# Paced early weight splits, four chunk buffers, spread bias broadcasts and a turned mask product in a two-model forward pass

## The chip, the cores and the metric

One core of one Trainium2 chip runs the kernel. The metric is the device time of one execution in microseconds (us), less being better; a run before the change and a run after it are measured in the same way. The core has a matrix engine (TensorE, PE in the profile; its weight loads are shown apart as PEld), a vector engine (VectorE, DVE), an activation engine (ScalarE, ACT), a general engine (GpSimd, POOL) and a synchronisation engine (SyncE, SP). SP issues most of the DMAs here, POOL and ACT a few.

## The reference, cut to what matters

Two models run one after the other on one sequence of 512 tokens of width 1024, in float32.

```python
def first_block(x, ...):                       # layer 0: short convolution, layer 1: NSA attention
    for layer in range(2):
        h = rms_norm(x, norm_mix[layer])
        x = x + (short_conv_mixer(h, ...) if layer < 1 else nsa_mixer(h, ...))
        x = x + squared_relu_mlp(rms_norm(x, norm_mlp[layer]), mlp_w1[layer], mlp_w2[layer])
...
def ssd_chunked(x, dt, a, bmat, cmat):         # 5 chunks of 128 positions, 4 groups of 8 heads of 64
    cs = jnp.cumsum(dtc * a.reshape(SSD_GROUPS, SSD_HPG), axis=2)
    lmat = jnp.exp(jnp.where(causal, cs_t[..., :, None] - cs_t[..., None, :], -jnp.inf))
    cb = jnp.einsum('bclgn,bcsgn->bcgls', cc, bc)
    y_diag = jnp.einsum('bcgls,bcgrls,bcsgrp->bclgrp', cb, lmat, xdt)
    ...
    return (y_diag + y_off).reshape(bsz, lp, SSD_HEADS, SSD_HEADDIM)

def second_block(x, ...):                      # 16 meta tokens in front, then one layer
    h = h + valid_h * mixer_block(h, ...)      # SSD and sliding-window attention, gated and merged
    h = h + valid_h * conv_ffn(h, ...)
```

The bias of the attentions depends on the distance of two positions alone (`t5_bucket`), so a row of biases by distance per head is enough; every row of a tile takes it shifted by one.

## The kernel before, in words

**Products.** Activations lie with their 1024 features over eight tiles of 128 partitions and the 512 tokens along the free axis. A product keeps float32 accuracy by three products of rounded parts: every operand is split into a high part and a rest, and `mm3` (L305 is where it issues them) does high by high, rest by high and high by rest. `gemm` makes one 128-feature output tile from the k tiles of a weight in two halves of four (half a chunk each). A matmul reads its weights (the stationary operand) first: in the trace `mm<-hh,whi` has the moving operand's tile and then the weight's.

**The weight stream.** All big weights lie in one tensor of 362 chunks of 128x1024 float32 (512 KB), in the order of use. `Stream.pre` (from L178) is called ahead of each half: SP loads the chunk into `w32` (name `w` in the trace, two buffers, up to two chunks ahead, L188), ACT rounds a half into `whi` (L207, L200), and DVE makes `wlo = w - whi` (L209); whi and wlo have four buffers and run up to three halves ahead of the half in use.

**The early split.** `Stream.ahead` (L147 to L175) is called once for a chunk of the stream, from the tenth chunk on, in layer A and in both MLPs. At three calls of four it takes one later chunk out of `todo` (those of the NSA attention, 96 to 132, and of the second model's mixer, 197 to 271: 112 in all): POOL loads it into `aw` (L161), ACT rounds it to `ah` (L172; L168 where a scale is folded in, in pieces), DVE makes `al` (L173, L169), and POOL stores `al` to a DRAM tensor `dlo` (L174). When the chunk's turn comes, SP loads `wlo` from `dlo` (L197) and DVE is spared. Tiles `aw` and `al` have two buffers, `ah` one.

**The order.** The program is written in loops, and a scheduler that plays a timeline orders each engine's instructions; what is pinned (`keep_in_program_order`) stays in the order written. The engines run their own lists strictly in that order.

**The stages.** By the trace: layer A (short convolution, `layer_a`) to 224 us, MLP 0 to 587, NSA attention to 940, MLP 1 to 1315, preparation and window attention of the second model to 1510, its SSD cores (with the attention's output and further projections laid between as filler) to some 1910, merge to 2090, feed-forward layer to 2474.

**The bias broadcasts.** In layer A `biases` (from L600) makes one row of biases per head (`line`, in DRAM), and POOL then copies each of the 16 rows to 128 rows of DRAM three times (`sk1`, `sk2`, `sk3`; 320, 192 and 72 KB; L622, named `sk<-line` in the trace), with a pitch one longer than the row, so that later reads come out shifted.

**The SSD core.** Per group of eight heads, `core` first adds the part of earlier chunks into `y4` (positions on partitions, L1527). Per head it then makes the decay mask: PE spreads the head's cumulated sums over 128 partitions (`s<-csT,indr`, a 64x512 product, L305), ACT takes the difference and its exponent (L1542, L1544: tile `L`, two buffers), POOL multiplies by the shared matrix (L1545), `split` makes `Mh` and `Ml` (one buffer each). For each of four chunks, PE takes Mh and Ml as weights of 128 columns (`u<-xd,Mh`, 128 columns moved; `u<-xd,Ml`, 64). DVE adds the two halves of `u` into `y4` (L1555, L1556). After every second head PE turns `y4` (`o<-ckt,y`), and DVE adds it to `xs` with the skip term (L1562). PSUM holds two `u` tiles.

Of the kernel before, what the change touches and what calls it, by code (L numbers as in the profile page):

```python
# [19 lines left out]
P = 128  # L20
# [28 lines left out]
AHEAD0 = 10  # L49
# [76 lines left out]
class Stream:  # L126
# [13 lines left out]

    def scaled(self, half):
        g, ks = self.plan[half]
        n = 512 // len(ks)
        for i, k in enumerate(ks):
            yield slice(i * n, i * n + n), self.b.pv(g, k)

    def ahead(self):  # L147
        if self.ap is None or not self.todo or self.nd < AHEAD0:
            return
        self.owed += 3  # L150
        if self.owed < 4:
            return
        self.owed -= 4
        nc = self.b.nc
# [7 lines left out]
        if 2 * c in self.plan or 2 * c + 1 in self.plan:  # L162
            for o in range(2):
                e = slice(o * 512, o * 512 + 512)
                ws, hs, ls = w[:, e], h[:, e], l[:, e]
                parts = self.scaled(2 * c + o) if 2 * c + o in self.plan else [(slice(0, 512), 1.0)]
                for a, sc in parts:
                    nc.scalar.activation(out=hs[:, a], in_=ws[:, a], func=AF.Copy, scale=sc)  # L168
                    nc.vector.scalar_tensor_tensor(out=ls[:, a], in0=ws[:, a], scalar=sc, in1=hs[:, a].bitcast(F32),  # L169
                                                   op0=ALU.mult, op1=ALU.subtract)  # L170
        else:
            nc.scalar.activation(out=h, in_=w, func=AF.Copy)  # L172
            nc.vector.tensor_tensor(out=l, in0=w, in1=h.bitcast(F32), op=ALU.subtract)  # L173
# [10 lines left out]
    def pre(self, half):  # L184
        b, nc = self.b, self.b.nc
        while self.nd < min(self.nch, half // 2 + 2):
            t = self.pool.tile([P, 1024], F32, tag="w32", name="w32", bufs=2)
            nc.sync.dma_start(t, self.src[self.nd])  # L188
            self.w32[self.nd] = t
            self.nd += 1  # L190
# [41 lines left out]
class Builder:  # L232
# [230 lines left out]
    def first(self):  # L463
# [15 lines left out]
        with ExitStack() as c:  # L479
# [3 lines left out]
            self.st.ap = c.enter_context(tc.tile_pool(name="ahead", bufs=1))  # L483
# [3 lines left out]
            if self.stop == "a":  # L487
                return
            self.mlp("mlp_w1_0", "mlp_w2_0", "g_mlp0")
# [17 lines left out]
    def layer_a(self):  # L507
# [14 lines left out]
        for f in range(KD):  # L522
            pcs = []
            for part in (1, 2, 0):
                if f == 0 and part:
                    p = (p1, p2)[part - 1]
                else:
                    p = self.ps1()
                    self.gemm([(p, XS)], "a_w_in", 0, part * 1024 + f * 128, hs)
                pcs.append(p)  # L530
# [26 lines left out]
        for m in range(KD):  # L557
            p = self.ps1()
            self.gemm([(p, slice(0, 512))], "a_w_out", 0, m * 128, ys)
            x = self.xs[m]  # L560
# [39 lines left out]
    def biases(self):  # L600
# [19 lines left out]
        for h in range(16):  # L620
            for sk, a, n in ((self.sk1, 0, 640), (self.sk2, OH_A, 384), (self.sk3, OH_A + 384, 144)):
                nc.gpsimd.dma_start(sk[h:h + 1, :].rearrange("o (q w) -> (o q) w", w=n + 1)[:, 0:n],  # L622
                                    self.line[h:h + 1, a:a + n].to_broadcast([128, n]))
# [719 lines left out]
    def dt_unit(self, tp):  # L1343
# [60 lines left out]
        self.csT = ap.tile([64, W], F32R, name="csT")  # L1404
        pt = self.mmb()
        for c in range(4):
            self.tr(pt[0:32, c * 128:c * 128 + 128], cs[:, c * 32:c * 32 + 32])
        nc.scalar.activation(out=self.csT[0:32, 16:528], in_=pt[0:32], func=AF.Copy)
        nc.vector.tensor_tensor(out=self.csT[32:64, 16:528], in0=pt[0:32], in1=self.csT[0:32, 16:528].bitcast(F32),
                                op=ALU.subtract)  # L1410
# [18 lines left out]
    def ssd(self, c):  # L1429
# [13 lines left out]
        def core(g):  # L1443
# [77 lines left out]
            for cx in range(4):  # L1521
# [8 lines left out]
                if cx < 3:  # L1530
# [4 lines left out]
                    nc.vector.tensor_tensor(out=prev, in0=prev, in1=po, op=ALU.add)  # L1535
            for i in range(8):
                h = 8 * g + i
                s = self.sb()
                self.mm(s, self.indr[0:64, h:h + 1].to_broadcast([64, P]), self.csT[:, XS], True, True)
                L = t5("L", 2, "L")  # L1540
                for cx in range(4):
                    nc.scalar.activation(out=L[:, cx * 128:cx * 128 + 128], in_=s[:, cx * 128:cx * 128 + 128], func=AF.Relu,  # L1542
# [4 lines left out]
                self.split(Mh, Ml, L)  # L1547
                u = self.ub()
                for cx in range(4):
                    cc = slice(cx * 128, cx * 128 + 128)  # L1550
                    self.mm(u[:, cc], Mh[:, cc], xds[cx][:, i].rearrange("p a b -> p (a b)"), True, False)
                    self.mm(u[:, cx * 128:cx * 128 + 64], Ml[:, cc], xds[cx][:, i, 0, :], False, True)
                uv = u.rearrange("p (c b) -> p c b", b=128)
                yv = y4[:, :, i * 64:i * 64 + 64]
                nc.vector.tensor_tensor(out=yv, in0=uv[:, :, 0:64], in1=yv, op=ALU.add)  # L1555
                nc.vector.tensor_tensor(out=yv, in0=uv[:, :, 64:128], in1=yv, op=ALU.add)  # L1556
                if i % 2:
                    t = i // 2
                    po = self.ob()
                    for cx in range(4):  # L1560
                        self.tr(po[:, cx * 128:cx * 128 + 128], y4[:, cx, t * 128:t * 128 + 128])
                    nc.vector.scalar_tensor_tensor(out=xs[t][:, XS], in0=xs[t][:, XS], scalar=self.pv("dsk", 4 * g + t),  # L1562
                                                   in1=po, op0=ALU.mult, op1=ALU.add)
# [317 lines left out]
```

## Time and profile before, and how to read it

| | us |
|---|---|
| median of three runs | 2486.36 |
| the three runs | 2483.63, 2486.36, 2491.55 |
| the profiled execution, its own time | 2476.05 |
| its span, first to last instruction | 2474.3 |
| PE busy | 2391.7 |
| DVE busy | 1624.5 |
| ACT busy | 1231.0 |
| POOL busy | 471.5 |

A profile has one execution. Its tables give busy time per engine, the work in stretches of the span, what an engine waited for, and the start of each instruction. In a stretch of uniform products, the number of matmuls by the spacing of an undisturbed stretch is the time PE needs; what the stretch took beyond that was lost. Idle time of an engine that is not the bottleneck costs nothing by itself.

### The profile page before, as it was taken

What the parts mean: (1) busy time and instruction counts of PE and PEld (TensorE: products, weight loads), DVE (VectorE), ACT (ScalarE), POOL (GpSimd) and SP (SyncE); (2) the same over time, 40 slices, a digit from 0 to 9 for tenths busy, and PEclk for the clock granted to TensorE, in tenths of its full rate; (3) what the DMA queues carried; (4) which work ended last, traced back from release to release, by engine and by line L of the source; (5) the groups of instructions that cost most, each with busy time, mean ns of one, the idle gap of its engine ahead of it and who ended that gap; (6) DMA issues with size and microseconds to landing.
All of it is one profiled execution on the core that took longest, in us unless ns stands there. A gap on an engine that the chain in (4) does not pass through costs nothing.

```text
span 2474.3 us, 38734 instructions
## 1 busy us (share of the span) xinstructions
PE 2391.7 (97%) x14273; PEld 2078.8 (84%) x14273; DVE 1624.5 (66%) x3293; ACT 1231.0 (50%) x2431; POOL 471.5 (19%) x657
## 2 busy tenths in 40 slices
PE   7999999999899999999999999999999999999997
PEld 5777777887787777777888999999999999998996
DVE  8657855543777768746636895569776566864873
ACT  6436543333677765434344776556555334432442
POOL 2333221001333322221022222122322100000001
PEclk9999999999999999999999999999999999999998
DMA  7898886335743347887335354543335452333322
GB/s 277 271 266 289 303 306 223 95 117 166 242 129 93 120 144 255 297 283 278 103 94 195 114 149 148 166 152 121 125 125 162 141 196 86 95 94 94 92 88 77
DMA packets 151739, 418.93 MB, mean 169 GB/s; under 512 B 22603, under 2 KB 29003, under 8 KB 151499
## 3 DMA queue, kind: packets, MB, share of 16 engines
q1 hardware_dynamic: 115024, 287.70, 36.3%
q0 software_dynamic: 35392, 127.49, 15.4%
q8 instruction: 112, 1.84, 0.3%
q10 hardware_dynamic: 1132, 1.26, 0.2%
q14 instruction: 79, 0.65, 0.1%
HBM read 340.62 MB, written 83.23 MB: 171 GB/s over the span
## 4 chain that ended last, share of the span: by engine, by line
PE 67%; issue 17%; POOL 5%; DMA 4%; DVE 4%; ACT 2%; POOLq 0%; DVEq 0%; SPq 0%; ACTq 0%
PE mm L305 53%; PE g L305 4%; PE o L305 3%; PE s L305 2%; DMA sk<-line 2%; POOL aw L161 2%; POOL dlo L174 2%; PE u L305 1%; DMA aw<-in_ws_dram 1%; PE pt L309 1%; PE u L309 1%; DVE e L728 1%; DMA w<-in_ws_dram 1%; ACT ph L313 0%; POOL acc L339 0%
## 5 line engine op out<-in xcount | busy, mean ns | idle before, releaser
L305 PE MATMUL mm<-hh,whi 128*128 128x258 f32 (+2 forms) x2464 | 799.0, 325 | 23.2 <-ACT hh L353 11.6
L305 PE MATMUL mm<-hh,wlo 128*128 128x258 f32 (+2 forms) x2464 | 798.7, 324 | 4.5 <-DVE wlo L209 4.5
L305 PE MATMUL mm<-hl,whi 128*128 128x258 f32 (+2 forms) x2464 | 798.8, 324 | 4.3 <-DVE hl L354 4.3
L207 ACT ACTIVATE whi<-w 128x512 fp32r<-128x512 f32 x500 | 308.5, 626 | 499.1 <-PE mm L305 322.7
L305 PEld LDWEIGHTS mm<-hh,whi 128*128 128x128 f32 x2464 | 464.5, 189 | 70.5 <-ACT hh L353 15.4
L209 DVE TENSOR_TENSOR wlo<-w,whi 128x512 fp32r<-128x512 f32 x498 | 347.9, 702 | 242.7 <-ACT whi L207 235.3
L305 PEld LDWEIGHTS mm<-hh,wlo 128*128 128x128 f32 x2464 | 465.3, 189 | 48.8 <-DVE wlo L209 7.4
L305 PEld LDWEIGHTS mm<-hl,whi 128*128 128x128 f32 x2464 | 465.1, 189 | 46.8 <-DVE hl L354 6.1
L305 PE MATMUL mm<-a,whi 128*128 128x512 f32 (+1 forms) x699 | 275.5, 395 | 5.1 <-ACT whi L207 4.7
L305 PE MATMUL mm<-a,wlo 128*128 128x512 f32 (+1 forms) x699 | 276.2, 395 | 3.8 <-DVE wlo L209 3.5
L305 PE MATMUL mm<-b,whi 128*128 128x512 f32 (+1 forms) x699 | 275.3, 394 | 1.8 <-DVE b L314 1.8
L173 DVE TENSOR_TENSOR al<-aw,ah 128x1024 fp32r<-128x1024 f32 x91 | 111.4, 1224 | 125.8 <-ACT ah L172 125.6
L172 ACT ACTIVATE ah<-aw 128x1024 fp32r<-128x1024 f32 x91 | 96.3, 1059 | 176.9 <-DMA aw<-in_ws_dram 169.2
L305 PEld LDWEIGHTS mm<-a,wlo 128*128 128x128 f32 x699 | 132.6, 190 | 38.5 <-DVE wlo L209 8.8
L305 PEld LDWEIGHTS mm<-a,whi 128*128 128x128 f32 x699 | 132.5, 189 | 37.4 <-ACT whi L207 6.9
L200 ACT ACTIVATE whi<-w 128x512 fp32r<-128x512 f32 x182 | 114.0, 630 | 97.1 <-PE mm L305 88.4
L305 PEld LDWEIGHTS mm<-b,whi 128*128 128x128 f32 x699 | 132.6, 190 | 32.2 <-DVE b L314 2.4
L174 POOL DMA_DIRECT2D dlo<-al x112 | 60.5, 540 | 440.1 <-DVE al L173 324.0
L305 PE MATMUL mm<-oh,whi 128*128 128x258 f32 (+1 forms) x400 | 123.8, 311 | 2.3 <-ACT oh L313 2.1
L305 PE MATMUL mm<-ol,whi 128*128 128x258 f32 (+1 forms) x400 | 124.2, 310 | 0.3 <-DVE ol L314 0.3
L305 PE MATMUL mm<-oh,wlo 128*128 128x258 f32 (+1 forms) x400 | 123.4, 308 | 0.0
L305 PEld LDWEIGHTS mm<-oh,whi 128*128 128x128 f32 x400 | 76.8, 193 | 7.7 <-ACT oh L313 2.4
(541 smaller groups left out, 4292.3 us busy)
## 6 DMA issues: line engine op xcount, KB each, us to landing
w<-in_ws_dram SPq DMA_DIRECT2D x361, 512.0 KB, 4.1
aw<-in_ws_dram POOLq DMA_DIRECT2D x112, 512.0 KB, 6.3
dlo<-al POOLq DMA_DIRECT2D x112, 512.0 KB, 4.3
wlo<-dlo SPq DMA_DIRECT2D x224, 256.0 KB, 2.9
sk<-line POOLq DMA_DIRECT2D x16, 320.0 KB, 9.4
bias<-sk SPq DMA_DIRECT2D x16, 256.0 KB, 3.2
sk<-line POOLq DMA_DIRECT2D x16, 192.0 KB, 9.7
x<-xs SPq DMA_DIRECT2D x8, 264.0 KB, 2.8
```

The lines of the kernel that those rows point to most:

```text
L161: nc.gpsimd.dma_start(w, self.src[c])
L172: nc.scalar.activation(out=h, in_=w, func=AF.Copy)
L173: nc.vector.tensor_tensor(out=l, in0=w, in1=h.bitcast(F32), op=ALU.subtract)
L174: nc.gpsimd.dma_start(self.dlo[c], l.bitcast(F32))
L200: nc.scalar.activation(out=h[:, a], in_=src[:, a], func=AF.Copy, scale=sc)
L207: nc.scalar.activation(out=h, in_=src, func=AF.Copy)
L209: eng.tensor_tensor(out=l, in0=src, in1=h.bitcast(F32), op=ALU.subtract)
L305: self.nc.tensor.matmul(out, l, r, start=start, stop=stop)
L309: self.nc.tensor.transpose(out, in_, self.ident[0:n, 0:n])
L728: (nc.gpsimd if g in EPOOL else nc.vector).tensor_tensor(out=ev[64 * q:64 * q + 64, :, g, 0:nn], in0=src[:, q, 4 * jh:4 * jh + 4, b:b + nn ...
```

## The change

- **Pace.** `ahead` takes part in seven calls of eight, without a first chunk to wait for, and `st.ap`, the pool that turns it on, is set behind layer A. So no early split lies in layer A; 56 of 64 chunks of each MLP carry one, which is again 112. Its ACT instructions are pinned.
- **Four chunk buffers.** In the MLPs, chunks whose number leaves 0 or 1 by four go into `ax`, two buffers in the pool of the early split, and the load runs four chunks ahead instead of two.
- **Broadcasts.** The 48 `sk<-line` DMAs go to ACT's queue, pinned, two behind each product of layer A (`skew_out`), all of sk1 first.
- **Decay rows.** The cumulated sums go to DRAM once (`csd`), and SP broadcasts a head's row to `L` (256 KB, three buffers), in place of PE's product `s`.
- **Mask product.** The eight heads' `y4` goes through PE and the skip term ahead of the heads. Per head and chunk PE takes the head's values as weights of 64 columns (xh twice, xl once) and moves 128 columns of Mh, Ml, Mh: 12 matmuls, where there were 8. DVE adds `u` (64 partitions by 512) into `xs` once.

```diff
@@ -48,3 +48,4 @@
 MIX_CH = (197, 272)
-AHEAD0 = 10
+MLP_CH = ((34, 96), (135, 197))
+AHEAD = (7, 8)
 
@@ -140,2 +141,5 @@
 
+    def aux(self, c):
+        return self.ap is not None and any(a <= c < b for a, b in MLP_CH)
+
     def scaled(self, half):
@@ -147,9 +151,9 @@
     def ahead(self):
-        if self.ap is None or not self.todo or self.nd < AHEAD0:
+        if self.ap is None or not self.todo:
             return
-        self.owed += 3
-        if self.owed < 4:
+        self.owed += AHEAD[0]
+        if self.owed < AHEAD[1]:
             return
-        self.owed -= 4
-        nc = self.b.nc
+        self.owed -= AHEAD[1]
+        nc, pin = self.b.nc, self.b.tc.keep_in_program_order
         c = self.todo.pop(0)
@@ -167,3 +171,3 @@
                 for a, sc in parts:
-                    nc.scalar.activation(out=hs[:, a], in_=ws[:, a], func=AF.Copy, scale=sc)
+                    pin(nc.scalar.activation(out=hs[:, a], in_=ws[:, a], func=AF.Copy, scale=sc))
                     nc.vector.scalar_tensor_tensor(out=ls[:, a], in0=ws[:, a], scalar=sc, in1=hs[:, a].bitcast(F32),
@@ -171,3 +175,3 @@
         else:
-            nc.scalar.activation(out=h, in_=w, func=AF.Copy)
+            pin(nc.scalar.activation(out=h, in_=w, func=AF.Copy))
             nc.vector.tensor_tensor(out=l, in0=w, in1=h.bitcast(F32), op=ALU.subtract)
@@ -185,4 +189,7 @@
         b, nc = self.b, self.b.nc
-        while self.nd < min(self.nch, half // 2 + 2):
-            t = self.pool.tile([P, 1024], F32, tag="w32", name="w32", bufs=2)
+        while self.nd < min(self.nch, half // 2 + (4 if self.aux(half // 2 + 3) else 2)):
+            if self.aux(self.nd) and self.nd % 4 < 2:
+                t = self.ap.tile([P, 1024], F32, tag="ax", name="ax", bufs=2)
+            else:
+                t = self.pool.tile([P, 1024], F32, tag="w32", name="w32", bufs=2)
             nc.sync.dma_start(t, self.src[self.nd])
@@ -482,3 +489,2 @@
             self.pst = lambda: ps.tile([P, 512], F32, tag="st", bufs=1, name="st")
-            self.st.ap = c.enter_context(tc.tile_pool(name="ahead", bufs=1))
             with ExitStack() as c2:
@@ -488,2 +494,3 @@
                 return
+            self.st.ap = c.enter_context(tc.tile_pool(name="ahead", bufs=1))
             self.mlp("mlp_w1_0", "mlp_w2_0", "g_mlp0")
@@ -529,2 +536,3 @@
                     self.gemm([(p, XS)], "a_w_in", 0, part * 1024 + f * 128, hs)
+                    self.skew_out()
                 pcs.append(p)
@@ -559,2 +567,3 @@
             self.gemm([(p, slice(0, 512))], "a_w_out", 0, m * 128, ys)
+            self.skew_out()
             x = self.xs[m]
@@ -619,6 +628,13 @@
         self.sk3 = self.dr.tile([16, 128 * 145], F32, name="sk3")
-        for h in range(16):
-            for sk, a, n in ((self.sk1, 0, 640), (self.sk2, OH_A, 384), (self.sk3, OH_A + 384, 144)):
-                nc.gpsimd.dma_start(sk[h:h + 1, :].rearrange("o (q w) -> (o q) w", w=n + 1)[:, 0:n],
-                                    self.line[h:h + 1, a:a + n].to_broadcast([128, n]))
+        self.skews = [(h, sk, a, n) for sk, a, n in ((self.sk1, 0, 640), (self.sk2, OH_A, 384), (self.sk3, OH_A + 384, 144))
+                      for h in range(16)]
+
+    skews = ()
+
+    def skew_out(self):
+        for _ in range(min(2, len(self.skews))):
+            h, sk, a, n = self.skews.pop(0)
+            self.tc.keep_in_program_order(
+                self.nc.scalar.dma_start(sk[h:h + 1, :].rearrange("o (q w) -> (o q) w", w=n + 1)[:, 0:n],
+                                         self.line[h:h + 1, a:a + n].to_broadcast([128, n])))
 
@@ -1403,3 +1419,3 @@
         nc.scalar.activation(out=self.dec, in_=pe[:, 0:160], func=AF.Exp)
-        self.csT = ap.tile([64, W], F32R, name="csT")
+        self.csT = ap.tile([64, 16], F32R, name="csT")
         pt = self.mmb()
@@ -1407,5 +1423,6 @@
             self.tr(pt[0:32, c * 128:c * 128 + 128], cs[:, c * 32:c * 32 + 32])
-        nc.scalar.activation(out=self.csT[0:32, 16:528], in_=pt[0:32], func=AF.Copy)
-        nc.vector.tensor_tensor(out=self.csT[32:64, 16:528], in0=pt[0:32], in1=self.csT[0:32, 16:528].bitcast(F32),
-                                op=ALU.subtract)
+        csr = tp.tile([32, 512], F32, name="csr")
+        nc.scalar.activation(out=csr, in_=pt[0:32], func=AF.Copy)
+        self.csd = self.dr.tile([32, 512], F32, name="csd")
+        nc.sync.dma_start(self.csd, csr)
         pt = self.mmb()
@@ -1535,9 +1552,14 @@
                     nc.vector.tensor_tensor(out=prev, in0=prev, in1=po, op=ALU.add)
+            for t in range(4):
+                po = self.ob()
+                for cx in range(4):
+                    self.tr(po[:, cx * 128:cx * 128 + 128], y4[:, cx, t * 128:t * 128 + 128])
+                nc.vector.scalar_tensor_tensor(out=xs[t][:, XS], in0=xs[t][:, XS], scalar=self.pv("dsk", 4 * g + t),
+                                               in1=po, op0=ALU.mult, op1=ALU.add)
             for i in range(8):
                 h = 8 * g + i
-                s = self.sb()
-                self.mm(s, self.indr[0:64, h:h + 1].to_broadcast([64, P]), self.csT[:, XS], True, True)
-                L = t5("L", 2, "L")
+                L = t5("L", 3, "L")
+                nc.sync.dma_start(L, self.csd[h:h + 1, :].to_broadcast([P, 512]))
                 for cx in range(4):
-                    nc.scalar.activation(out=L[:, cx * 128:cx * 128 + 128], in_=s[:, cx * 128:cx * 128 + 128], func=AF.Relu,
+                    nc.scalar.activation(out=L[:, cx * 128:cx * 128 + 128], in_=L[:, cx * 128:cx * 128 + 128], func=AF.Relu,
                                          scale=-1.0, bias=self.cs[:, cx * 32 + h:cx * 32 + h + 1])
@@ -1547,2 +1569,3 @@
                 self.split(Mh, Ml, L)
+                t, e = divmod(i, 2)
                 u = self.ub()
@@ -1550,15 +1573,8 @@
                     cc = slice(cx * 128, cx * 128 + 128)
-                    self.mm(u[:, cc], Mh[:, cc], xds[cx][:, i].rearrange("p a b -> p (a b)"), True, False)
-                    self.mm(u[:, cx * 128:cx * 128 + 64], Ml[:, cc], xds[cx][:, i, 0, :], False, True)
-                uv = u.rearrange("p (c b) -> p c b", b=128)
-                yv = y4[:, :, i * 64:i * 64 + 64]
-                nc.vector.tensor_tensor(out=yv, in0=uv[:, :, 0:64], in1=yv, op=ALU.add)
-                nc.vector.tensor_tensor(out=yv, in0=uv[:, :, 64:128], in1=yv, op=ALU.add)
-                if i % 2:
-                    t = i // 2
-                    po = self.ob()
-                    for cx in range(4):
-                        self.tr(po[:, cx * 128:cx * 128 + 128], y4[:, cx, t * 128:t * 128 + 128])
-                    nc.vector.scalar_tensor_tensor(out=xs[t][:, XS], in0=xs[t][:, XS], scalar=self.pv("dsk", 4 * g + t),
-                                                   in1=po, op0=ALU.mult, op1=ALU.add)
+                    o, xh, xl = u[0:64, cc], xds[cx][:, i, 0, :], xds[cx][:, i, 1, :]
+                    self.mm(o, xh, Mh[:, cc], True, False)
+                    self.mm(o, xh, Ml[:, cc], False, False)
+                    self.mm(o, xl, Mh[:, cc], False, True)
+                yr = xs[t][64 * e:64 * e + 64, XS]
+                nc.vector.tensor_tensor(out=yr, in0=u[0:64], in1=yr, op=ALU.add)
             return xs
```

The order on ACT at the start of the program, first before and then in the change (hh is the first split of x, ah the early split, sq the squares for the norm).

```order
L207 ACTIVATE whi<-w_81 128x512
L168 ACTIVATE ah<-aw,pkt 128x128 x8
L353 ACTIVATE hh<-x,pkt 128x512
L334 ACTIVATE sq<-x 128x512
L168 ACTIVATE ah<-aw,pkt 128x256 x4
L353 ACTIVATE hh<-x,pkt 128x512
```

```order
L214 ACTIVATE whi<-w_81 128x512
L360 ACTIVATE hh<-x,pkt 128x512
L341 ACTIVATE sq<-x 128x512
L360 ACTIVATE hh<-x,pkt 128x512
L341 ACTIVATE sq<-x 128x512
L214 ACTIVATE whi<-w_81 128x512
```

The early split's pieces no longer stand ahead of the first hh, on which PE's first product waits.

ACT's order in the change about the middle of layer A, where the broadcasts now lie (cv and yh belong to the convolution; each sk row is a DMA that ACT issues).

```order
L214 ACTIVATE whi<-w_677 128x512 x2
L214 ACTIVATE whi<-w_714 128x512 x2
L553 ACTIVATE cv<-v,pkt 128x512
L214 ACTIVATE whi<-w_767 128x512
L638 DMA sk_493<-line 128x640 x12
L320 ACTIVATE yh<-o 128x512
L214 ACTIVATE whi<-w_767 128x512
L638 DMA sk_493<-line 128x640 x2
L214 ACTIVATE whi<-w_804 128x512 x2
L638 DMA sk_493<-line 128x640 x2
```

The first twelve stand in one block between two halves of one chunk's whi; from there on they come in pairs.

SP's order in the change in the second of the four SSD cores (L is the decay row's broadcast, wlo a rest read back from dlo).

```order
L204 DMA wlo<-dlo 128x512 x2
L195 DMA w_17697<-in_ws_dram 128x1024
L204 DMA wlo<-dlo 128x512
L1562 DMA L<-csd 128x512
L204 DMA wlo<-dlo 128x512
L195 DMA w_17768<-in_ws_dram 128x1024
L1562 DMA L<-csd 128x512
L204 DMA wlo<-dlo 128x512 x2
```

An L load, which needs a free L buffer, stands in the same queue ahead of loads of the weight stream.

## Rows read from the trace of the kernel before

**Rows 1.** The page: busy time by engine, and the chain that ended last.

```profile
PE 2391.7 (97%) x14273; PEld 2078.8 (84%) x14273; DVE 1624.5 (66%) x3293; ACT 1231.0 (50%) x2431; POOL 471.5 (19%) x657
...
PE 67%; issue 17%; POOL 5%; DMA 4%; DVE 4%; ACT 2%; POOLq 0%; DVEq 0%; SPq 0%; ACTq 0%
```

**Rows 2.** Stretches of the span: width, busy us (and instructions) by engine, granted clock, DMA.

```profile
core 0: us, PE busy (x) PEld busy (x) DVE busy (x) ACT busy (x) POOL busy (x), PEclk, DMA share, GB/s
0.00:36.00 36.00, 17.92 (x56) 12.21 (x57) 26.25 (x58) 22.92 (x48) 13.50 (x19) 0.95 0.76 268
...
100.00:170.00 70.00, 65.13 (x272) 51.34 (x271) 33.97 (x54) 20.01 (x36) 27.27 (x52) 0.98 0.99 259
...
246.00:328.00 82.00, 78.84 (x338) 62.56 (x337) 65.81 (x93) 41.87 (x62) 17.20 (x33) 1.00 0.85 301
328.00:400.00 72.00, 69.75 (x291) 53.66 (x289) 36.59 (x46) 28.75 (x39) 15.79 (x31) 1.00 0.89 311
400.00:550.00 150.00, 149.80 (x647) 121.56 (x648) 78.40 (x117) 50.70 (x82) 4.83 (x5) 1.00 0.36 113
...
1030.00:1170.00 140.00, 131.24 (x536) 102.70 (x535) 75.52 (x98) 55.30 (x77) 28.43 (x54) 0.96 0.81 288
1170.00:1315.00 145.00, 144.58 (x624) 116.97 (x622) 69.73 (x111) 57.12 (x104) 17.91 (x14) 1.00 0.35 108
...
1510.00:1910.00 400.00, 397.17 (x3022) 373.89 (x3021) 278.34 (x570) 227.63 (x475) 100.81 (x79) 0.99 0.44 139
```

**Rows 3.** Timeline of the start: start us, duration us, engine, line, operation, [idle before, releaser].

```profile
3.54 0.63 ACT L207 ACTIVATE whi<-w 128x512 fp32r<-128x512 f32 x1 [0.74 <-DMA w<-in_ws_dram]
...
4.54 3.97 SPq L468 DMA_DIRECT2D x<-in_x_dram  x4
7.93 2.44 ACT L168 ACTIVATE ah<-aw,pkt 128x128 fp32r<-128x128 f32 x8 [3.76 <-DMA aw<-in_ws_dram]
...
10.28 0.70 ACT L353 ACTIVATE hh<-x,pkt 128x512 fp32r<-128x512 f32 x1
...
11.04 1.22 PE L305 MATMUL mm<-hh,whi 128*128 128x512 f32 x2 [11.04 <-ACT hh L353]
```

**Rows 4.** Waits of PE from 0 to 36 us: in total, times, longest.

```profile
PE mm L305 <- DVE hl L354: 4.3, 2, 2.2
PE mm L305 <- DVE wlo L209: 1.9, 1, 1.9
```

**Rows 5.** Timeline of POOL's queue in layer A.

```profile
101.57 4.19 POOL L622 DMA_DIRECT2D sk<-line  x8 [2.95 <-DMA line<-la]
106.85 0.52 POOL L622 DMA_DIRECT2D sk<-line  x1 [1.09 <-DMA sk<-line]
...
113.35 1.56 POOL L622 DMA_DIRECT2D sk<-line  x3 [2.68 <-DMA sk<-line]
```

**Rows 6.** Groups of instructions: busy us, mean ns of one, idle before (releaser).

```profile
L173 DVE TENSOR_TENSOR al<-aw,ah 128x1024 fp32r<-128x1024 f32 x17 | 20.8, 1223 | 13.8 <-ACT ah L172 13.8
L209 DVE TENSOR_TENSOR wlo<-w,whi 128x512 fp32r<-128x512 f32 x28 | 18.8, 683 | 2.7 <-ACT whi L207 2.7
L587 DVE SCALAR_TENSOR_TENSOR q<-u 128x512 f32<-128x512 f32 x16 | 11.0, 685 | 0.1
...
L172 ACT ACTIVATE ah<-aw 128x1024 fp32r<-128x1024 f32 x91 | 96.3, 1059 | 176.9 <-DMA aw<-in_ws_dram 169.2
```

**Rows 7.** DMA issues by tile: KB each, median us from issue to landing (whole span).

```profile
w<-in_ws_dram SPq DMA_DIRECT2D x361, 512.0 KB, 4.1
aw<-in_ws_dram POOLq DMA_DIRECT2D x112, 512.0 KB, 6.3
```

**Rows 8.** Groups in 1510 to 1910 us, the SSD cores: busy us, mean ns, idle before.

```profile
L305 PE MATMUL u<-xd,Mh 128*128 128x128 f32 x128 | 31.4, 283 | 2.8 <-DVE y L1556 2.8
...
L305 PE MATMUL s<-csT,indr 64*128 64x512 f32 x32 | 16.2, 511 | 0.0
```

**Rows 9.** Timeline of PE: the ends of a run of seven mask products, and of five with 64-column weights.

```profile
1591.79 0.19 PE L305 MATMUL u<-xd,Ml 128*128 128x64 f32 x1
...
1592.48 0.37 PE L305 MATMUL mm<-hh,whi 128*128 128x264 f32 x1
...
657.24 0.22 PE L305 MATMUL mm<-phl,phw 128*64 128x128 f32 x1
...
657.54 0.33 PE L305 MATMUL mm<-whi,eh 128*128 128x256 f32 x1
```

**Rows 10.** Tile L, all instructions: ns min, median, max, first and last start.

```profile
L1544 ACT ACTIVATE L<-L x32: 614/644/687, 1525.1 to 1895.9; 128x512 f32<-128x512 f32 x32
```

## The prediction

> **What bounds the kernel now.** The page comes first: PE is busy 2391.7 of 2474.3 us and leads the chain that ended last with 67%; DVE, the next, has 66% [rows 1]. So only what takes work from PE, or a wait of PE, counts. The second view is the table of stretches. In 400 to 550 us, where hardly an early split runs, 647 matmuls take 150 us, 0.2318 us each at full clock [rows 2]. With that price the loss of a stretch is its width less its matmuls times 0.2318: 36 - 56 x 0.2318 = 23.0 us in 0 to 36, 7.0 in 100 to 170, 3.65 in 246 to 328, 4.55 in 328 to 400, 15.8 in 1030 to 1170 (536 matmuls in 140 us, granted clock 0.96), and 0.4 in 1170 to 1315 [rows 2]. The losing stretches have the early split; the quiet stretches of the same MLPs lose nothing. The sum below is made against the profiled execution's 2476.05 us; the median of the runs, 2486.36, lies 10.3 us (0.4%) above it, and the forecast is the median less the gain.
>
> **1. The start.** PE's first product comes at 11.04 us, behind hh, which ACT began at 10.28. Ahead of hh on ACT stands the first early split: eight pieces, 2.44 us, that first waited 3.76 us for aw [rows 3]. In the change hh stands there, behind the first whi, which ended at 4.17. Without the 2.44 and 3.76, hh could begin some 6 us earlier. Two waits for hl (4.3) and one for wlo (1.9) follow, on a DVE that has the al pieces ahead of them [rows 4]; they should mostly go, 5 more. That makes **-11**. The bounds: the last four x tiles are issued from 4.54 to 8.51 us [rows 3], so PE may catch up with the loads, and only the 6 stay; or the clock, 0.95 in this stretch, recovers too: -6 to -14.
>
> **2. The broadcasts.** Before, POOL issues them; the stretch loses 7.0 us at a DMA share of 0.99 [rows 2]. In the change ACT issues the first twelve in a block, and ACT keeps its order: behind them yh and half a whi. POOL's rows give the price: eight issues take 4.19 us, the ninth waited 1.09 us for an earlier one to land, and the twelfth, the first of three from 113.35, was out 12.3 us after the first began [rows 5]. PE has three halves of weights in stock. A half is 12 matmuls, so 3 x 12 x 0.2318 = 8.3 us. The block alone would cost 12.3 - 8.3 = 4 us; SP's loads no longer run against early splits and all 48 broadcasts together, and the later pairs come 5.6 us apart. Of the 7.0, 5 should remain with the block: **-2**. The ends: -7 when the landings are fast enough for the stock to cover the block, +6 when it takes twice 8.3 us.
>
> Here a rule of the pages speaks against the part. The row shows that POOL's issue alone takes 4.19 us for eight [rows 5], which no other engine waited for. The Trainium skill (DMA: Bandwidth & Descriptors, "Issuing engines are not separate DMA queues") says that DMAs of all engines end on the same 16 DMA engines, and that another issuing engine saves only the issue time. By it the move as such would gain nothing and its term would be 0, not -2.
>
> **3. MLP 0 and MLP 1.** Before, the split runs as fast as its loads allow: ACT waited 169.2 us for aw in all, in order, with whi behind [rows 6]; DMA moves 288 to 311 GB/s at a share of 0.81 to 0.89 [rows 2], and a load of aw takes 6.3 us [rows 7]. In the change a chunk (24 matmuls, 5.56 us) carries 7/8 of a split: 512 KB for w and 7/8 of 1024 KB for aw and dlo make 1.44 MB in 5.56 us, 259 GB/s, below what these rows moved; and w is requested four chunks ahead, 22 us, against a landing of 4.1 [rows 7]. So whi should no longer be late. What is late next is DVE: in the first product of an MLP a chunk asks of it two wlo (683 ns), u, q and b (taken at q's 685 each) and 7/8 of an al (1223): 1.37 + 2.06 + 1.07 = 4.5 us of 5.56 [rows 6], 81%. That fits, with short waits where a scaled al comes in pieces. I take the losses down from 8.2 to 3 in MLP 0 (**-5**, from -8 to 0) and from 15.8 to 3 in MLP 1 (**-13**, from -16 to 0). The ahead work that moves from layer A into MLP 0's quiet stretch is hidden there by DVE's 78.4 of 150 us [rows 2]; if that cover were gone, each al would cost up to its 1.22 us.
>
> **4. The SSD cores.** PE is busy 397 of 400 us here, DVE 278 [rows 2]: matmuls are the whole price. Removed: 32 products `s`, 16.2 us [rows 8], and 256 mask products. Seven of these start from 1591.79 to the next other product at 1592.48 [rows 9], 0.099 us each, 25.2 us for all. Added: 32 x 12 = 384 products with 64-column weights and 128 columns moved. The nearest rows are five such products from 657.24 to the next product's start at 657.54 [rows 9], 0.060 us each, so 384 x 0.060 = 23.0 us. The balance is 16.2 + 25.2 - 23.0 = 18.4; of PE's two waits for DVE's y, 2.8 us [rows 8], a part should go with one add in place of two: **-19**. The ends: at the 0.099 of the present products, 38.0 us, the gain is 3.4; with all waits gone, 21.2.
>
> On this one a page would give another price. The rows show 0.06 us a step for 64-column weights, in a run of five only. The Trainium skill (TensorE: Matmul & The Clock Gate, "Back-to-back issue gap") puts a sustained stream of weight load and 128-column matmul at about 81 ns each. By it the estimate would be 31 us for the new products and a gain of some 10.
>
> Costed at nothing: the L loads (32 x 256 KB = 8.4 MB over 400 us, 21 GB/s beside 139 [rows 2]); the adds and ACT's steps, under DVE's 278 and ACT's 228 of 400 us; the turns of y4 that move ahead of the heads, the same in number. The scheduler orders the other stages anew; for that I allow 6 us either way and take 0.
>
> **The sum.** -11 - 2 - 5 - 13 - 19 = -50: the profile would come to 2426, the runs to 2486.4 - 50 = **2436**.
>
> **The rivals.**
>
> *A. The MLPs stay as they are.* DVE or the loads are the bound in them, and an even pace only spreads the loss: 56 splits in each MLP, where the early chunks of MLP 0 had fewer. For it: ACT is in order, and aw still lands after 6.3 us [rows 7]. Against it: 259 GB/s and 81%. Without the 18 us: 2486.4 - 32 = 2454.
>
> *B. The broadcasts are not spread.* The block of twelve holds ACT, and later w loads wait for slow landings behind them. At +6 for the block and as much again behind it, 12 in place of -2, the gain is 36: 2450. For it: the ninth issue's wait [rows 5].
>
> *C. The turned product gains little.* If a weight load of 64 columns costs a step of 0.099 in this mix, part 4 gives 3: 2470 - 18, that is 2486.4 - 34 = 2452.
>
> *D. Slower: SP's queue in the cores.* 29 of the 32 L loads wait for a free L buffer, with wlo and w queued behind them on SP. The heads follow each other (1895.9 - 1525.1) / 31 = 12 us apart [rows 10], and PE's stock of three halves is 8.3 us or more here. If an L load stands for the stock and x us more, 29x is lost; from x = 1.7 the change's 50 us are gone. At x = 2.5 it is 2486.4 - 50 + 72 = 2508. For it: three buffers are taken by heads that are not yet multiplied. Against it: a head is done long before the third one behind it is asked for.
>
> **How the numbers follow.** The forecast, 0.60; A 0.13, B 0.10, C 0.11, D 0.06. What a measurement can tell from no change is about 0.3%, 7.5 us: faster is below 2478.9. A, B and C all end below that even in pairs (A with C: 2470); A, B and C together come to 2484, which with D's milder forms makes 0.05 for the same, and 0.04 for slower; 0.91 stays for faster. The lower end sums the better ends: -14 - 7 - 8 - 16 - 21 = -66, and not all at once: 2486 - 66 = 2420, less 6 for the new order: 2414. The upper end takes in two rivals together, 2470, and the order's 6: 2476.
>
> **What would show it.** Right: PE's first product before 7 us; no whi waits in 940 to 1170; the new u products some 23 us; in layer A one wait of a few us on whi or yh behind the block. Wrong: PE waits for wlo all through the MLPs at a DVE near 90%; u steps of 0.08 or more; SP's queue standing at an L load while PE waits for wlo.

## The result and the profile after

| | before | after |
|---|---|---|
| median of the runs, us | 2488.34 (4 runs) | 2442.97 (4 runs, 2439.07 to 2445.16) |
| ratio to before | | 0.9829, 95% interval 0.9805 to 0.9852 |
| the profiled execution's own time | 2476.05 | 2439.07 |
| span | 2474.3 | 2437.3 |

The change makes the kernel faster by 1.7%, 42.5 us by the ratio. The profiled execution of before was faster than every other run of it in this study (the next is 2483.55), so the two traces differ by 37.0 us only; the traces tell where these 37 lie and nothing of the rest.

The products of the weight stream (`mm`, `g` and the like with whi or wlo, 12057 in both traces) are the measure: where the n-th of them starts in either trace shows what was won up to there.

| n-th product of the stream | lies in | before | after | difference | since the row above |
|---|---|---|---|---|---|
| 0 | first product | 11.0 | 6.8 | -4.3 | -4.3 |
| 100 | layer A, early | 48.5 | 36.4 | -12.1 | -7.9 |
| 400 | layer A, middle | 123.5 | 126.8 | +3.3 | +15.4 |
| 600 | layer A, near its end | 177.3 | 173.0 | -4.3 | -7.6 |
| 1600 | MLP 0, quiet part | 423.0 | 406.4 | -16.6 | -12.4 |
| 3000 | NSA attention | 879.2 | 862.4 | -16.8 | -0.2 |
| 4000 | MLP 1 | 1167.8 | 1134.0 | -33.9 | -17.1 |
| 5000 | window attention | 1370.4 | 1336.6 | -33.9 | 0.0 |
| 9000 | behind the SSD cores | 2027.8 | 1992.4 | -35.4 | -1.5 |
| 12000 | near the end | 2447.5 | 2412.2 | -35.3 | 0.1 |

So the start and both MLPs won some 42 us, layer A's middle lost 15 and got half of that back, and the SSD cores, from which the forecast took its largest term, brought 1.5.

The stretches of the profile after, by its own stages (columns as in [rows 2]):

```profile
0.00:36.00 36.00, 26.57 (x103) 20.22 (x104) 24.69 (x60) 17.90 (x30) 7.52 (x9) 1.00 0.58 189
...
84.00:120.00 36.00, 24.24 (x91) 18.57 (x90) 11.14 (x18) 5.96 (x10) 0.00 (x0) 0.86 0.78 183
...
240.00:582.00 342.00, 341.12 (x1471) 274.54 (x1470) 229.30 (x362) 168.14 (x285) 65.94 (x122) 1.00 0.77 264
...
925.00:1282.00 357.00, 356.12 (x1537) 288.33 (x1536) 236.46 (x343) 169.54 (x256) 77.44 (x124) 1.00 0.75 257
...
1480.00:1878.00 398.00, 382.81 (x3165) 367.14 (x3164) 285.58 (x540) 229.96 (x480) 105.27 (x79) 1.00 0.55 165
```

103 products in the first 36 us stand against 56 before. The MLPs run without a gap: 1471 products x 0.2318 = 341.0 of 342 us. In 84 to 120 us PE is busy 24 of 36 us, at a granted clock of 0.86. In the SSD cores PE idles 15.2 of 398 us, where it idled 2.8 of 400 before.

ACT's timeline in layer A shows the block of twelve broadcasts, and the chain of work shows what followed from it (start, duration):

```profile
84.73 16.52 ACTq L638 DMA_DIRECT2D sk<-line  x12
101.30 0.63 ACT L320 ACTIVATE yh<-o 128x512 fp32r<-128x512 f32 x1 [17.96 <-DMA sk<-line]
...
115.12 0.63 ACT L214 ACTIVATE whi<-w 128x512 fp32r<-128x512 f32 x1 [6.59 <-DMA w<-in_ws_dram]
```

```profile
90.36 1.74 ACTq L638
92.11 0.03 issue
92.13 12.09 DMA sk<-line
...
104.30 10.72 DMA w<-in_ws_dram
...
115.12 0.64 ACT whi L214
```

```profile
PE mm L312 <- ACT whi L214: 11.8, 2, 8.6
```

ACT stood 16.5 us in its queue, yh and half a whi behind it. A load of w on SP went out only at 104.3: its buffer came free at 103.3, with the wlo behind the late whi, and a broadcast's landing held it 1.0 us more. It took 10.7 us to land: the second wait, 3.2 us. The last fence is PE's line among its waits from 0 to 240 us.

Behind each of the two waits the products start some 0.43 us apart instead of 0.23, seven after the first and nine after the second, at a granted clock of about 0.5 (1.2 GHz):

```profile
102.50:105.65 3.15, 3.15 (x7) 2.36 (x8) 1.40 (x4) 1.15 (x2) 0.00 (x0) 0.50 0.81 224
115.80:119.50 3.70, 3.70 (x9) 2.72 (x10) 3.70 (x7) 2.26 (x4) 0.00 (x0) 0.54 0.70 137
```

Against 0.2318 us each that adds 1.5 and 1.7 us, so the block's account is 8.6 + 3.2 + 1.5 + 1.7 = 15.0 of the 15.4 us.

In the SSD cores, the groups and waits of PE from 1477 to 1908 us:

```profile
L312 PE MATMUL u<-Mh,xd 128*64 128x128 f32 x256 | 33.8, 227 | 9.6 <-ACT Mh L320 9.5
L312 PE MATMUL u<-Ml,xd 128*64 128x128 f32 x128 | 25.1, 226 | 1.5 <-DVE Ml L321 1.5
```

```profile
PE u L312 <- ACT Mh L320: 9.5, 10, 1.6
PE g L312 <- DVE dh L415: 2.6, 1, 2.6
PE mm L312 <- DVE u L1345: 2.0, 3, 1.6
PE u L312 <- DVE Ml L321: 1.5, 4, 0.6
PE u L312 <- ACT xdh L320: 1.2, 1, 1.2
```

By the distance from each start to PE's next, the old core's products took 17.0 (s), 15.3 and 9.8 us (u), the new u takes 17.2 + 8.1 = 25.3 us: 16.7 us of work are gone. But PE waits where it hardly did. These are the stretches from product 5000 to product 9000, before and after:

```profile
1370.40:2027.80 657.40, 651.40 (x5109) 624.19 (x5108) 468.71 (x1046) 378.08 (x824) 141.24 (x127) 0.99 0.46 146
```

```profile
1336.60:1992.40 655.80, 634.32 (x5204) 614.09 (x5204) 476.41 (x1013) 376.37 (x825) 145.48 (x127) 0.99 0.52 159
```

PE idles 6.0 us in the first and 21.5 in the second. These 15.5 us more leave 1.2 of the 16.7, and 1.5 were measured. The timeline of SP and ACT in the third core shows a loop:

```profile
1776.63 0.32 SPq L1562 DMA_DIRECT2D L<-csd  x1
1783.01 0.32 SPq L1562 DMA_DIRECT2D L<-csd  x1
```

```profile
1780.46 1.28 ACT L1564 ACTIVATE L<-L,cs 128x128 f32<-128x128 f32 x4 [2.30 <-DVE cvt L1351]
1781.64 0.61 ACT L320 ACTIVATE Mh<-L 128x512 fp32r<-128x512 f32 x1
...
1787.20 1.28 ACT L1564 ACTIVATE L<-L,cs 128x128 f32<-128x128 f32 x4 [1.82 <-DMA L<-csd]
1788.39 0.61 ACT L207 ACTIVATE whi<-w 128x512 fp32r<-128x512 f32 x1
1788.91 0.61 ACT L320 ACTIVATE Mh<-L 128x512 fp32r<-128x512 f32 x1
```

A head's Ml frees an L buffer; the load for the third head behind it goes out at once (1776.63) and lands some 4 us later; ACT's four steps on it stand in ACT's list ahead of the next head's Mh (1781.64), whose Ml then frees the next buffer (1783.01): 6.4 us for a turn, though that next head's own L was ready at 1778.6, behind POOL's product (start 1777.20, 1.37 us), and the last product that read the mask buffer before it started at 1777.41.

### The profile page after: what moved, and what is told of

Its sections match the earlier page's. It is cut to its first block, busy times and chain, and to the rows that moved or that the text cites. A ratio compares the mean times of both kernels' runs of the same rounds, so it can differ in the third digit from the quotient of the medians.

```text
span 2437.3 us, 38984 instructions
## 1 busy us (share of the span) xinstructions
PE 2360.5 (97%) x14369; PEld 2067.7 (85%) x14369; DVE 1643.9 (67%) x3260; ACT 1234.4 (51%) x2431; POOL 450.0 (18%) x609
## 4 chain that ended last, share of the span: by engine, by line
PE 80%; DVE 7%; DMA 5%; ACT 4%; issue 2%; ACTq 0%; POOL 0%; SPq 0%; POOLq 0%; DVEq 0%
PE mm L312 69%; PE g L312 3%; PE o L312 3%; DMA L<-csd 3%; PE s L312 2%; PE pt L316 1%; DMA w<-in_ws_dram 1%; ACT L L1564 1%; PE u L316 1%; DVE e L744 1%; DVE pl L321 1%; DVE cvt L1351 1%; DVE Ml L321 1%; PE u L312 1%; ACT ph L320 1%
## 5 line engine op out<-in xcount | busy, mean ns | idle before, releaser
L312 PE MATMUL mm<-hh,whi 128*128 128x258 f32 (+2 forms) x2464 | 796.9, 324 | 26.4 <-ACT whi L214 12.4
L214 ACT ACTIVATE whi<-w 128x512 fp32r<-128x512 f32 x378 | 237.8, 631 | 487.6 <-PE mm L312 362.4
L216 DVE TENSOR_TENSOR wlo<-w,whi 128x512 fp32r<-128x512 f32 x376 | 263.8, 703 | 218.2 <-ACT whi L214 209.3
L214 ACT ACTIVATE whi<-ax 128x512 fp32r<-128x512 f32 x122 | 76.9, 631 | 146.6 <-PE mm L312 146.5
L207 ACT ACTIVATE whi<-w 128x512 fp32r<-128x512 f32 x182 | 111.8, 623 | 62.4 <-PE mm L312 55.6
L216 DVE TENSOR_TENSOR wlo<-ax,whi 128x512 fp32r<-128x512 f32 x122 | 83.8, 688 | 70.2 <-ACT whi L214 70.0
```

The lines of the kernel that those rows point to most:

```text
L207: nc.scalar.activation(out=h[:, a], in_=src[:, a], func=AF.Copy, scale=sc)
L214: nc.scalar.activation(out=h, in_=src, func=AF.Copy)
L216: eng.tensor_tensor(out=l, in0=src, in1=h.bitcast(F32), op=ALU.subtract)
L312: self.nc.tensor.matmul(out, l, r, start=start, stop=stop)
```

## The experiments

Ratios are to the kernel before, run beside each experiment; the changed kernel has 0.9829 (0.9805 to 0.9852).

**1. The SSD core as before.** The changed kernel with before's head loop and csT.

> The changed kernel with the SSD core of before (decay row by PE, Mh and Ml as weights, adds into y4), all else as changed. Theory: the 17 us of PE work that the new core saves (42.0 us of product steps removed, 25.3 added, by the two traces) is given back in new waits of PE for ACT's Mh, 9.5 us, and other waits, so undoing the core costs about nothing: within 3 us of the changed kernel, ratio to the kernel before about 0.982 to 0.984, the PE waits for Mh in the cores gone. Rival (the prediction's part 4): the new core is worth 19 us, so this kernel would be 15 to 20 us slower than the changed one, ratio about 0.990.

Ratio 0.9816 (0.9791 to 0.9841), 2445.31 us. PE's waits in the cores are the two for y again, 2.8 us. The theory held: the new core, with 16.7 us less work, is worth nothing that can be measured.

**2. Six L buffers.**

```diff
-                L = t5("L", 3, "L")
+                L = t5("hw", 3, "L") if i % 2 else t5("L", 3, "L")
```

> The changed kernel, but every second head's L takes one of the three buffers that the core's preparation uses for ph, pl, wh and wl, so six buffers in all. Theory: L loads that wait for a buffer, and so land late ahead of ACT's Mh, cause the waits of PE in the cores; with six buffers ACT's 54.8 us of waits for L fall below 15, PE's 9.5 us for Mh below 3, and the time falls by 8 to 14 us against the changed kernel. Rival: the heads' chain over ACT, POOL and DVE is too long by itself (POOL's product 1.3 us, ACT's order); then the waits for Mh stay near 9 us and the time within 3 us.

Ratio 0.9827 (0.9797 to 0.9856), 2447.20 us: no gain. PE's waits from 1477 to 1920 us:

```profile
PE s L312 <- DVE cl L321: 3.8, 1, 3.8
PE u L312 <- ACT Mh L320: 3.1, 5, 1.0
PE u L312 <- DVE Ml L321: 2.1, 3, 1.6
```

The wait for Mh fell from 9.5 to 3.1, but ACT still waited 42.8 us for L, and other operands became late. More buffers alone were not the cure; the expectation missed.

**3. Broadcasts later.** They start in the sixth round of layer A instead of the third, when the row has landed, and end in MLP 0.

```diff
-                    self.skew_out()
+                    if f > 4:
+                        self.skew_out()
...
                     self.gemm([(p, XS)], w1, 0, half * 2048 + m * 128, hs)
+                    self.skew_out()
```

> The changed kernel, but the broadcasts start three products later, from the sixth round of layer A, when the row has landed, and the last ones go into MLP 0, so that no block of twelve stands in ACT's order, only pairs. Theory: the block held ACT 16.5 us, and PE lost 8.6 and 3.2 us in two waits for whi and some 3 us at half clock behind them; these go, so 12 to 16 us less than the changed kernel, and no PE wait over 1 us between 60 and 200 us. Rival: it is the broadcasts' traffic, not their block, that delays the loads of w (landing up to 10.7 us), and then a wait of 3 us or more comes back at the later place and the gain is 6 us or less.

Ratio 0.9748 (0.9722 to 0.9774), 2426.94 us, and PE has no wait between 60 and 200 us. The n = 400th product starts at 111.7 instead of 126.8 us. The block was the whole loss; the traffic, in pairs, costs PE no wait.

**4. The split not pinned.**

```diff
-            pin(nc.scalar.activation(out=h, in_=w, func=AF.Copy))
+            nc.scalar.activation(out=h, in_=w, func=AF.Copy)
```

(and the same for the scaled pieces)

> The changed kernel with ACT's part of the early split not pinned, so that the scheduler may place it. Theory: the pinned order makes the pace (in the kernel before, splits ran 5 us apart though three in four chunks had one, 7.4 us); without it they bunch again and the DMA-bound waits for whi and wlo come back in both MLPs: 5 to 20 us slower than the changed kernel. Rival: the four chunk buffers absorb it, and the time stays within 3 us.

Ratio 1.0005 (0.9992 to 1.0019), 2492.05 us: with this alone the whole gain is gone, more than was expected. The start keeps its gain (12.0 us at n = 100); against the changed kernel the trace loses 24 us around MLP 0 (n = 800 to 2300) and 26 around MLP 1 (3000 to 4500). Its waits in MLP 0, first of ACT, then of PE:

```profile
ACT ah L176 <- DMA aw<-in_ws_dram: 73.8, 28, 5.5
```

```profile
PE mm L312 <- ACT whi L214: 7.7, 8, 2.8
PE mm L312 <- DVE wlo L216: 6.5, 10, 1.1
```

The scheduler put ten splits into 50 us in both MLPs, as in the kernel before, and ACT stood in front of ah waiting for its load, with whi behind it. In the changed kernel ACT's wait of this kind in MLP 0 is small, and PE has one wait of 0.9 us in MLP 0 and none in MLP 1:

```profile
ACT ah L172 <- DMA aw<-in_ws_dram: 2.6, 3, 2.0
```

**5. Two chunk buffers.** `MLP_CH = ()`.

> The changed kernel without the two added chunk buffers (loads two chunks ahead, as before); pace and pinning stay. Theory: the pinned pace alone removes the waits of the MLPs (an unpinned one brought all of them back though it had four buffers), so within 4 us of the changed kernel, ratio to before 0.981 to 0.985. Rival: with a landing of up to 6 us, two chunks ahead are too few beside the split, and waits of PE for whi return in both MLPs, 10 us or more.

Ratio 0.9816 (0.9788 to 0.9844), 2445.68 us, PE's only wait in each MLP 0.9 us. The four buffers bring nothing that can be measured.

**6. The kernel before, pinned.** Three lines of the old kernel, the same as in experiment 4 the other way.

> The kernel before with ACT's part of the early split pinned and nothing else changed (pace three of four, from the tenth chunk, in layer A too, broadcasts on POOL, old SSD core). Theory: pinning is what makes a pace hold; it takes the pieces away from ahead of the first hh and spreads the splits to 7.4 us, so that the start (-12) and most of both MLPs' waits (-25) are won, ratio 0.984 to 0.990; the waits of layer A between 100 and 170 us stay. Rival: it is the new pace and the later start that count, and pinning the old program wins under 10 us, ratio above 0.996.

Ratio 0.9811 (0.9793 to 0.9829), 2444.39 us: as fast as the whole change. Its trace has the first product at 7.0 us and is 10.9 us ahead of before at n = 100, 14.8 at n = 1600, 31.6 from n = 4000 to the end. In the MLPs PE waits 0.9 us in each; layer A keeps its waits. ACT waits 20.0 us for aw in all, where it waited 179.5 before. A little more than expected.

**7. The decay row by PE.** The turned product stays, `s` comes back, L has two buffers.

> The changed kernel with the decay row made by PE's product again (17.0 us of steps in the trace before) and two L buffers, the turned mask product kept. Theory: the loop that makes the heads of a core follow at 6.3 to 7 us goes over the load (a buffer freed behind Ml, 3.8 us to land, ACT's four steps on it, and only then the next head's Mh, which stands behind them in ACT's order). Without the load PE's waits for Mh in the cores fall from 9.5 us to under 3, and the time stays within 5 us of the changed kernel although PE has 17 us more to do. Rival: the waits come from Mh and Ml having one buffer each; then they stay at 8 us or more and the kernel is 13 us or more slower than the changed one.

Ratio 0.9816 (0.9791 to 0.9840), 2445.02 us. PE's waits in the cores:

```profile
PE mm L312 <- DVE u L1345: 2.2, 3, 1.3
PE u L312 <- DVE Ml L321: 1.8, 1, 1.8
PE g L312 <- DVE dl L415: 0.8, 1, 0.8
PE u L312 <- ACT Mh L320: 0.4, 1, 0.4
```

PE's work for the decay row is back (32 products, 14.8 us by their starts in this trace, 17.0 before) and the waits for Mh are gone: the load of the decay row bought one with the other. It also shows that the turned product alone moves nothing (26.0 us here for 25.1 before, at the ratio of experiment 1).

**8. Two pairs of mask buffers**, with the later broadcasts.

```diff
-                Mh, Ml = t5("Mh", 1, "Mh", F32R), t5("Ml", 1, "Ml", F32R)
+                if i % 2:
+                    Mh, Ml = t5("bt", 2, "Mh", F32R), t5("bt", 2, "Ml", F32R)
+                else:
+                    Mh, Ml = t5("Mh", 1, "Mh", F32R), t5("Ml", 1, "Ml", F32R)
```

> The changed kernel with the later broadcasts of the earlier run, and with a second pair of buffers for Mh and Ml (odd heads use the two buffers that the core's preparation has for bth and btl). Theory (single mask buffers as a cause): waits for Mh fall below 4 us and the time is 5 us or more under the run with later broadcasts alone, 2427. Rival (the load's loop): the loop does not run over the mask buffers, so the waits stay near 9 us and the time within 3 us of 2427.

Ratio 0.9716 (0.9691 to 0.9740), 2420.44 us, 6.5 under experiment 3. The two intervals overlap in part, but the traces put the gain in the cores: from product 5000 to 9000 this one takes 649.5 us and that of experiment 3 656.7. PE's waits in the cores now:

```profile
PE u L316 <- DVE xs L1584: 3.8, 2, 2.4
PE u L312 <- DVE Ml L321: 1.9, 2, 1.4
PE u L312 <- ACT Mh L320: 1.8, 4, 0.8
```

The wait does hang on the mask buffers, and the rival's premise was wrong: with a second pair 19 of the 32 heads get their Mh before the head in front is multiplied, which one pair does not allow. But in the turn shown above the one buffer was free 4 us before Mh, and what stood ahead of it was ACT's order. That order changed with the second pair too. How much comes from the buffer itself and how much from the new order is not shown.

**9. Six L buffers as well.**

> The same with six L buffers as well. Theory: with both loosened the heads of a core are free of each other; PE's waits in the cores fall under 6 us in all (18 in the changed kernel) and 8 to 12 us of the turned product's 17 come out, about 2417. Rival: PE's waits move to other operands of the cores (with six L buffers alone they went to cl, y and u), and the time stays within 3 us of 2427.

Ratio 0.9716 (0.9693 to 0.9739), 2420.87 us: the same as experiment 8. Its one trace ends 4.9 us earlier; the runs do not show it. The waits that remain, 11.9 us against the 6 expected, are spread over many operands (Mh 5.2, u 3.3): the expectation missed.

**10. Broadcasts on POOL** in the changed kernel, in before's order.

> The changed kernel with the 48 broadcasts on POOL's queue again, in before's order. Theory: POOL has nothing else to do in layer A now, so its waits for landings hold nobody up and the block's 12 to 15 us are won as with the later broadcasts, 2427 to 2432; the traffic alone, with no early split beside it, costs under 3 us. Rival: 48 broadcasts one after another crowd out the loads of w (which landed after 9.3 us before), and PE waits for whi 4 us or more, 2435 or above.

Ratio 0.9785 (0.9767 to 0.9803), 2438.23 us: between theory and rival, nearer to the rival. PE's waits from 60 to 200 us:

```profile
PE mm L312 <- ACT whi L214: 3.9, 2, 2.1
```

Nobody stands behind the queue, but 48 broadcasts together delay the loads (w landed after 11.3 us from 80 to 140 us, 7.1 in the changed kernel), and nearly half of what experiment 3 won is lost again. The block on ACT was worse than POOL; spread pairs on ACT are better than both.

**11. The same with two pairs of mask buffers.**

> The same with the second pair of buffers for Mh and Ml. Theory: the two gains add, as the one lies in layer A and the other in the cores: 5 to 8 us under the run before it, 2420 to 2426. Rival: the scheduler's other order takes it back, within 3 us of that run.

Ratio 0.9741 (0.9717 to 0.9764), 2428.99 us: the two gains add, a little more than expected.

The fastest version is experiment 8 (or 9): 0.9716 to before, below both kernels.

## Why the prediction was right, and where its terms were not

The forecast was 50 us less; the ratio gives 42.5, and 2442.97 lies in the range. Term by term the agreement is partly luck: the MLPs' two terms were too small, the broadcasts' had the wrong sign, the SSD cores' came to next to nothing, and the misses partly cancelled.

**The start (-11): right.** -12.1 at n = 100. hh begins at 6.0 us and the first product at 6.8. The cause was right too, but either of two edits brings it: experiment 4 has it unpinned, with the split out of layer A (12.0), and experiment 6 has most of it from pinning, with the split still in layer A (10.9).

**The broadcasts (-2, from -7 to +6): wrong.** From n = 100 to 600 layer A lost 7.9 us net, 15.4 of them at the block. The step that failed is the block's price, 12.3 us from POOL's rows [rows 5]: on ACT it took 16.5. Its first four issues took 0.6 us each, the last seven 1.2 to 2.8. From the fifth on they were 1.8 us apart and the landings 2.0, so the block went at the pace of the landings. That it was slower than POOL's is probably a matter of size (twelve DMAs of 320 KB are 3.8 MB, POOL's first twelve had 2.3); no run varies the size alone. The end of +6 asked for 16.6 us of block, which it had; what was left out was the load of w that came out late behind it (3.2 us more) and the lower clock after both waits (3.2 us together). A premise of the -2 did not hold either: SP's loads had no early split to run against here before, as POOL, with the broadcasts in its queue, issued nothing of the split between 98.6 and 157.5 us. That SP would stand behind landings was named in rival B, and the measured 7.9 lies nearer to its 12 than to -2.

The Trainium skill (DMA: Bandwidth & Descriptors, "Issuing engines are not separate DMA queues") says that another issuing engine saves only the issue time. Experiment 10 agrees in this: the move to ACT won nothing by itself, and back on POOL the kernel is faster (0.9785 for 0.9829).

**The MLPs (-5 and -13): right in kind, too small.** They gave 12.4 and 17.1. I let 3 us of loss stay in each for DVE; 0.9 and 0 stayed, and 3.0 us between layer A and MLP 0, which no term counted, went too. DVE at 229 of 342 us was no bound, so rival A fell. The reason given (an even pace, loads four chunks ahead) is only half right: experiments 4, 5 and 6 show that in the MLPs the pinned order does it all, and that the four buffers do nothing. The 3.0 us ahead of MLP 0 are not pinning's: experiment 6 does not win them, and experiment 4, unpinned, does. What the pinned order changes is that ah stands behind loads that have landed, so ACT does not wait ahead of whi.

**The SSD cores (-19, from -21.2 to -3.4): wrong.** The work was priced well: 18.4 forecast, 16.7 measured. The step at 0.060 us from five products became 25.3 / 384 = 0.066, far from rival C's 0.099, so rival C fell. By the 81 ns of the Trainium skill (TensorE: Matmul & The Clock Gate, "Back-to-back issue gap") the estimate was 31 us. The measured 25.3 differs from it and decides. What failed is the sentence that matmuls are the whole price because PE was busy 397 of 400 us. With less to do, PE met the heads' chain over SP, ACT and DVE, and waited: 15.5 us more of idle time from product 5000 to 9000. Experiments 1 and 7 show both sides of it: the row by PE costs 15 to 17 us of work, the row by load costs as much in waits. Rival D had the place (an L load that waits for a buffer), but the wrong victim: PE never waited for wlo in the cores; what was late was the next head's mask.

**The order of the rest (0, 6 either way): right**, within 2 us.

## What to carry to other kernels

An instruction that waits for a DMA costs what stands behind it in its engine's list: where a scheduler moved the early split's ACT instructions (two lines of the program) ahead of their loads, holding them to the order of the program won as much as the whole change. A block of DMAs on a computing engine held it at the pace of their landings, not of their first issues; a few at a time, started when their source was there, cost nothing that could be measured. Work taken off the bound engine is worth only the slack of the chain that feeds it: look for the loop over a buffer's release, a load and an in-order list before counting the saved products.

## What was not expected of the hardware

Twelve DMAs of 320 KB, issued one behind another on ACT, held the engine 16.5 us, with single issues of 0.6 us at first and 1.2 to 2.8 us from the sixth on, and landed after 12.0 us (median of the 16), with only the loads of w beside them; in POOL's mixed order, also beside the loads of w alone, they had landed after 9.4. On POOL every issue stayed at 0.5 us, and the engine waited between the issues. After the 8.6 us in which PE stood, seven products came at the lower clock (7 starts in 3.15 us), and nine after the 3.2 us, which adds 1.5 and 1.7 us to these waits.
